# Splitting a load into 11 and 5 rows and holding back the first store in a rotary-embedding kernel on one core

## The chip, the cores and the metric

The kernel runs on one core of one Trainium2 chip. The metric is the device time of one execution in microseconds (us). Three runs of the kernel before gave 161.13, 161.54 and 161.68 us, with a median of 161.54 us.

## What is computed

The input `x` has the shape batch 16, sequence 512, heads 16, dim 64 in fp32. Of every head's 64 values, the first 32 are rotated by position-dependent factors and the last 32 are passed through. In the first 32, the quarters of 16 are the pair:

```python
x1, x2 = x[..., :32], x[..., 32:]
first  = x1[..., :16] * cos[..., :16] - x1[..., 16:] * sin[..., :16]
second = x1[..., :16] * sin[..., :16] + x1[..., 16:] * cos[..., :16]
out = concatenate([first, second, x2], axis=-1)
```

`cos` and `sin` are tables of 512 x 32, of which the first 16 columns are used. So 33.6 MB are read and 33.6 MB are written, and the arithmetic is four products, one difference and one sum for each rotated pair.

## The kernel before, in words

The 16 x 512 positions are cut into T = 4 tiles. Each tile holds 128 partitions x K = 16 positions, called rows here, of 16 heads x 64 values; a row of one partition is 4 KB, a tile is 8.4 MB. The buffer `ring` has room for NS = 3 tiles in SBUF, so tile 3 takes the place of tile 0 and can be loaded only when tile 0 has been stored. A tile is loaded into the buffer, its first half of every head is rotated in place, and the whole tile is stored, passed-through values included.

All loads and the stores of tiles 0, 1 and 3 are issued by SP (SyncE), in the order of the program: `load` (line 55) and `store` (line 58). The store of tile 2 is issued by POOL (GpSimd), which has a queue of its own. An issuing engine stops at an instruction that has to wait, and what stands behind it in the program waits too. On SP the order is: load 0, load 1, rows 8-16 of tile 2, store 0, rows 0-8 of tile 2, load 3, store 1, store 3.

The factors are loaded by two small transfers (lines 63 and 64), spread over partitions and repeated by VectorE (lines 73 to 86), until 21 us. From then on VectorE rotates. `rotate(t, lo, hi)` works on rows lo to hi of tile t, with four instructions: a multiplication by the sines into `b_t` in PSUM (line 96), a multiplication by the cosines in place (line 97), a subtraction for the first quarter (line 98) and an addition for the second (line 101). `b_t` has one buffer of KC = 8 rows, so no call takes more than 8 rows.

The order of the calls is written out by hand. Tiles 0, 1 and 3 are rotated in two calls of 8 rows. Tile 2 is rotated in rows 8-16, then 0-5 (KM = 5), then 5-8. Store 1 has an added dependency: it is held back until the addition of `rotate(2, 0, KM)`, called `near`, has ended, although tile 1 itself is ready earlier.

Of the kernel before, what the change touches and what calls it, by code (L numbers as in the profile page):

```python
# [1 line left out]

# [4 lines left out]


@with_exitstack
def kernel(  # L10
    ctx: ExitStack,
    tc: tile.TileContext,
    x: bass.AP,
    cos: bass.AP,
    sin: bass.AP,
    out: bass.AP,
):
    nc = tc.nc
    fp32 = mybir.dt.float32
    P = 128  # L20
    B, S, H, D = x.shape
    Q = D // 4
    HF = D // 2

    K = 16
    T = B * S // (P * K)
    PB = S // K
    REP = P // PB  # L30
    R = H * D
    NS = 3
    KC = K // 2
    KM = 5

    xf = x.rearrange("b s h d -> (b s h d)").rearrange("(t p f) -> t p f", t=T, p=P)
    of = out.rearrange("b s h d -> (b s h d)").rearrange("(t p f) -> t p f", t=T, p=P)
    cosf = cos.rearrange("(p k) j -> p (k j)", k=K)
    sinf = sin.rearrange("(p k) j -> p (k j)", k=K)

    const_pool = ctx.enter_context(tc.tile_pool(name="const", bufs=1))
    b_pool = ctx.enter_context(tc.tile_pool(name="bp", bufs=1, space=bass.MemoryType.PSUM))


    ring = const_pool.tile([P, NS, K, H, D], fp32)
    stage = const_pool.tile([P, 2, K, HF], fp32)
    spun = const_pool.tile([P, 2 * K, Q], fp32)
    packed = const_pool.tile([PB, 2 * K, Q], fp32)
    table = const_pool.tile([P, 2, K, 2, Q], fp32)

    def rows(t, lo, hi):
        return ring[:, t % NS, lo:hi].rearrange("p k h d -> p (k h d)")

    def load(t, lo=0, hi=K):
        return nc.sync.dma_start(out=rows(t, lo, hi), in_=xf[t, :, lo * R : hi * R])

    def store(t, lo=0, hi=K, queue=nc.sync):
        return queue.dma_start(out=of[t, :, lo * R : hi * R], in_=rows(t, lo, hi))  # L58


    nc.vector.memset(stage[:, :, :, 0:Q], 0.0)  # L61
    spread = stage.rearrange("(j b) t k i -> j b t (k i)", b=REP)
    nc.gpsimd.dma_start(out=spread[:, 0, 0], in_=cosf)  # L63
    nc.gpsimd.dma_start(out=spread[:, 0, 1], in_=sinf)  # L64
    load(0)
    load(1)
    load(2, KC, K)

    PQ = PB // REP
    nc.vector.stream_shuffle(  # L73
        out=spun[:],
        in_=stage.rearrange("p t k j -> p (t k) j")[:, :, 0:Q],
        mask=[j % PQ * REP for j in range(PB)],
    )
    for q in reversed(range(REP)):
        n = PQ * (q + 1)
        nc.vector.tensor_copy(out=packed[0:n], in_=spun[q * PB : q * PB + n])  # L80

    for r in range(REP):
        nc.vector.tensor_copy(  # L83
            out=table[r * PB : (r + 1) * PB].rearrange("p t k c j -> p (t k) c j"),
            in_=packed.unsqueeze(2).to_broadcast((PB, 2 * K, 2, Q)),
        )
    C = table[:, 0].rearrange("p k c j -> p k (c j)")
    Sn = table[:, 1].rearrange("p k c j -> p k (c j)")

    def rotate(t, lo, hi):  # L90
        x1 = ring[:, t % NS, lo:hi, :, 0:HF]
        c = C[:, lo:hi].unsqueeze(2).to_broadcast((P, hi - lo, H, HF))
        s = Sn[:, lo:hi].unsqueeze(2).to_broadcast((P, hi - lo, H, HF))
        b_full = b_pool.tile([P, KC, H, HF], fp32, name="b_t")
        b_t = b_full[:, 0 : hi - lo]
        nc.vector.tensor_mul(out=b_t, in0=x1, in1=s)  # L96
        nc.vector.tensor_mul(out=x1, in0=x1, in1=c)  # L97
        nc.vector.tensor_sub(  # L98
            out=x1[:, :, :, 0:Q], in0=x1[:, :, :, 0:Q], in1=b_t[:, :, :, Q:HF]
        )  # L100
        return nc.vector.tensor_add(  # L101
            out=x1[:, :, :, Q:HF], in0=x1[:, :, :, Q:HF], in1=b_t[:, :, :, 0:Q]
        )

    rotate(0, 0, KC)
    rotate(0, KC, K)
    store(0)
    load(2, 0, KC)
    load(3)
    rotate(1, 0, KC)  # L110
    rotate(1, KC, K)
    behind_loads = store(1)
    rotate(2, KC, K)
    near = rotate(2, 0, KM)
    rotate(2, KM, KC)
    store(2, queue=nc.gpsimd)

    tc.add_manual_dep(
        behind_loads.ins,
        near.ins.name,  # L120
        mybir.DependencyInfo(mybir.DependencyClass.Sync, mybir.DependencyReason.DATA),
        reason="the store follows the loads at the DMA engines",
    )
    rotate(3, 0, KC)
    rotate(3, KC, K)
    store(3)


# [1 line left out]
_INS = ['x', 'cos', 'sin']  # L130
_OUTS = [((16, 512, 16, 64), 'float32')]


# [23 lines left out]
```

## Time and profile before

| | |
|---|---|
| median of three runs | 161.54 us (161.13 to 161.68) |
| span of the profiled execution, first to last instruction | 159.5 us |
| median of the runs less that span | 2.04 us |
| VectorE busy | 112.9 us |
| POOL busy | 1.9 us |
| bytes moved | 67.24 MB, 422 GB/s over the span |
| store 0 issued | 49.92 us |
| store 1 issued | 98.90 us |
| store 2 issued (POOL) | 104.62 us |
| store 3 issued | 131.24 us |

The times in the lower half count from the first instruction of the profiled execution. The span is what the profiler saw between the first and the last instruction; the time of a run holds some more around it. In the profile DVE is VectorE and SPq is SP's instruction stream with its DMA issues; q1 is the queue that SP's transfers take and q0 that of POOL's. A DMA issue in a timeline is short: it hands the transfer over, and the transfer itself is seen in the DMA views and in the records of single packets.

### The profile page before, as it was taken

The page shows a single profiled execution, that of the slowest core. Times are in us where ns is not written, and L with a number is a line of the kernel's source. Part 1 is how long each engine was busy: PE and PEld are TensorE (multiplying, and loading weights), DVE is VectorE, ACT ScalarE, POOL GpSimd, SP SyncE. Part 2 cuts the span into 40 slices and gives each one's busy share as a digit, 9 for nine tenths or more (in the row PEclk, how much of TensorE's full clock was granted, in tenths as well). Part 3 has the DMA queues.
Part 4 walks back from the last instruction along what each step waited for, and adds up shares of the span by engine and source line. Part 5 has one row for each costly group of instructions (what it writes and reads, how often), then busy time and mean ns, then how long its engine had stood idle before and what let it go on. Part 6 is the DMA issues. An engine that isn't in the chain of part 4 may idle for free.

```text
span 159.5 us, 115 instructions
## 1 busy us (share of the span) xinstructions
DVE 112.9 (71%) x47; POOL 1.9 (1%) x7
## 2 busy tenths in 40 slices
DVE  1000959999999999999999999999999990000000
POOL 3000000000000000000000000010000000000000
DMA  7969979799699699699996996996996997999966
GB/s 263 542 263 542 444 345 526 345 444 526 271 493 551 279 510 526 263 394 411 510 526 263 526 526 263 526 526 263 526 526 263 526 460 329 526 394 394 526 263 263
DMA packets 1360, 67.24 MB, mean 422 GB/s; under 512 B 176, under 2 KB 176, under 8 KB 208
## 3 DMA queue, kind: packets, MB, share of 16 engines
q1 hardware_dynamic: 1152, 58.72, 85.7%
q0 software_dynamic: 208, 8.52, 12.4%
HBM read 33.69 MB, written 33.55 MB: 422 GB/s over the span
## 4 chain that ended last, share of the span: by engine, by line
DVE 61%; DMA 14%; issue 5%; DVEq 1%
DVE b_t L96 22%; DVE ring L97 22%; DMA ring<-in_x_dram 14%; DVE ring L101 10%; DVE ring L98 7%; DVEq L152 1%; DVEq L96 0%
## 5 line engine op out<-in xcount | busy, mean ns | idle before, releaser
L96 DVE TENSOR_TENSOR b_t<-ring,table 128x4096 f32<-128x4096 f32 (+2 forms) x9 | 35.6, 3959 | 2.1 <-DMA ring<-in_x_dram 1.8
L97 DVE TENSOR_TENSOR ring<-ring,table 128x4096 f32<-128x4096 f32 (+2 forms) x9 | 35.5, 3950 | 0.3
L98 DVE TENSOR_TENSOR ring<-ring,b_t 128x2048 f32<-128x2048 f32 (+2 forms) x9 | 18.4, 2049 | 0.3
L101 DVE TENSOR_TENSOR ring<-ring,b_t 128x2048 f32<-128x2048 f32 (+2 forms) x9 | 18.4, 2043 | 0.0
L73 DVE LOAD_MASK_SELECT spun<-stage x1 | 0.0, 14 | 14.4 <-DMA stage<-in_sin_dram 14.4
L83 DVE COPY table<-packed 32x1024 f32<-32x1024 f32 x4 | 2.7, 684 | 0.1
L58 POOL DMA_DIRECT2D out_dram<-ring x1 | 0.6, 562 | 101.7 <-DVE ring L101 101.7
L80 DVE COPY packed<-spun 32x512 f32<-32x512 f32 (+3 forms) x4 | 1.7, 416 | 0.1
L61 DVE MEMSET stage<- 128x512 f32 x1 | 0.5, 485 | 0.9 <-PEq L141 0.9
L73 DVE STREAM_SHUFFLE spun<-stage 128x512 f32<-128x512 f32 x1 | 0.7, 721 | 0.0
L63 POOL DMA_DIRECT2D stage<-in_cos_dram x1 | 0.6, 644 | 1.3 <-DVE stage L61 1.3
L64 POOL DMA_DIRECT2D stage<-in_sin_dram x1 | 0.5, 535 | 0.0
L141 POOL MEMSET const-bfloat16-1.0<- 128x1 bf16 x1 | 0.1, 102 | 0.0
L141 POOL MEMSET const-float32-0.0<- 128x1 f32 x1 | 0.1, 99 | 0.2 <-issue 0.2
L141 POOL MEMSET const-float32-1.0<- 128x1 f32 x1 | 0.1, 99 | 0.0
L141 POOL MEMSET const-uint8-127<- 128x1 uint8 x1 | 0.1, 99 | 0.0
## 6 DMA issues: line engine op xcount, KB each, us to landing
ring<-in_x_dram SPq DMA_DIRECT2D x2, 4096.0 KB, 40.7
stage<-in_cos_dram POOLq DMA_DIRECT2D x1, 64.0 KB, 9.0
stage<-in_sin_dram POOLq DMA_DIRECT2D x1, 64.0 KB, 13.3
ring<-in_x_dram SPq DMA_DIRECT2D x3, 29.0
out_dram<-ring SPq DMA_DIRECT2D x3, 27.4
out_dram<-ring POOLq DMA_DIRECT2D x1, 39.5
```

The costliest lines, as they stand in the source:

```text
L58: return queue.dma_start(out=of[t, :, lo * R : hi * R], in_=rows(t, lo, hi))
L61: nc.vector.memset(stage[:, :, :, 0:Q], 0.0)
L63: nc.gpsimd.dma_start(out=spread[:, 0, 0], in_=cosf)
L64: nc.gpsimd.dma_start(out=spread[:, 0, 1], in_=sinf)
L73: nc.vector.stream_shuffle(out=spun[:], in_=stage.rearrange("p t k j -> p (t k) j")[:, :, 0:Q], mask=[j % PQ * REP for j in range(PB)],)
L80: nc.vector.tensor_copy(out=packed[0:n], in_=spun[q * PB : q * PB + n])
L83: nc.vector.tensor_copy(out=table[r * PB : (r + 1) * PB].rearrange("p t k c j -> p (t k) c j"), in_=packed.unsqueeze(2).to_broadcast((PB, ...
L96: nc.vector.tensor_mul(out=b_t, in0=x1, in1=s)
L97: nc.vector.tensor_mul(out=x1, in0=x1, in1=c)
L98: nc.vector.tensor_sub(out=x1[:, :, :, 0:Q], in0=x1[:, :, :, 0:Q], in1=b_t[:, :, :, Q:HF])
L101: return nc.vector.tensor_add(out=x1[:, :, :, Q:HF], in0=x1[:, :, :, Q:HF], in1=b_t[:, :, :, 0:Q])
L152: with _tile.TileContext(nc) as tc:
```

## The change

Tile 2 is loaded as rows 5-16 (11 rows) ahead of store 0 and rows 0-5 (5 rows) behind it, instead of 8 and 8 rows. Tile 1 is rotated in calls of 7, 5 and 4 rows instead of 8 and 8. Store 0 gets an added dependency: it is held back until the first multiplication of tile 1 (line 96, over 7 rows) has ended. Tile 2 is rotated in rows 8-16, 3-8, 0-3 instead of 8-16, 0-5, 5-8; store 1 is held back, as before, until the addition of the second of these calls, which has 5 rows in both kernels. `rotate` now returns its first and its last instruction.

```diff
-    KM = 5
+    KA = 5
...
-    load(2, KC, K)
+    load(2, KA, K)
...
-        nc.vector.tensor_mul(out=b_t, in0=x1, in1=s)
+        first = nc.vector.tensor_mul(out=b_t, in0=x1, in1=s)
...
-        return nc.vector.tensor_add(
+        last = nc.vector.tensor_add(
             out=x1[:, :, :, Q:HF], in0=x1[:, :, :, Q:HF], in1=b_t[:, :, :, 0:Q]
         )
+        return first, last
...
-    store(0)
-    load(2, 0, KC)
+    first_store = store(0)
+    load(2, 0, KA)
     load(3)
-    rotate(1, 0, KC)
-    rotate(1, KC, K)
-    behind_loads = store(1)
-    rotate(2, KC, K)
-    near = rotate(2, 0, KM)
-    rotate(2, KM, KC)
+    begun, _ = rotate(1, 0, 7)
+    rotate(1, 7, 12)
+    rotate(1, 12, 16)
+    second_store = store(1)
+    rotate(2, 8, 16)
+    _, near = rotate(2, 3, 8)
+    rotate(2, 0, 3)
     store(2, queue=nc.gpsimd)
...
-    tc.add_manual_dep(
-        behind_loads.ins,
-        near.ins.name,
-        mybir.DependencyInfo(mybir.DependencyClass.Sync, mybir.DependencyReason.DATA),
-        reason="the store follows the loads at the DMA engines",
-    )
+    for behind, point in ((first_store, begun), (second_store, near)):
+        tc.add_manual_dep(
+            behind.ins,
+            point.ins.name,
+            mybir.DependencyInfo(mybir.DependencyClass.Sync, mybir.DependencyReason.DATA),
+            reason="the store follows the loads at the DMA engines",
+        )
```

## The prediction

> **What bounds the kernel now.** I read the page first, then the stretches, then the order of time around the waits that the change touches.
>
> The page's head, engine part and DMA queues:
>
> ```profile
> span 159.5 us, 115 instructions
> ...
> DVE 112.9 (71%) x47; POOL 1.9 (1%) x7
> ...
> DMA packets 1360, 67.24 MB, mean 422 GB/s; under 512 B 176, under 2 KB 176, under 8 KB 208
> ...
> q1 hardware_dynamic: 1152, 58.72, 85.7%
> q0 software_dynamic: 208, 8.52, 12.4%
> ```
>
> VectorE (DVE) is busy for 71% of the span, the two DMA queues for 85.7 + 12.4 = 98.1%. The kernel moves 67.24 MB and has hardly a moment in which the 16 DMA engines rest. The chain of waits gives VectorE 61%, but it stops at 131 us, where the last store is issued, and does not see that this store then stands behind other transfers. The view of stretches (columns: stretch, its us, VectorE busy, POOL busy, clock, DMA share, GB/s) shows the same:
>
> ```profile
> 4.00:50.00 46.00, 31.89 (x19) 0.00 (x0) 1.00 0.99 427
> ...
> 72.00:99.80 27.80, 27.52 (x12) 0.00 (x0) 1.00 1.00 434
> 99.80:158.20 58.40, 31.14 (x12) 0.56 (x1) 1.00 1.00 431
> ```
>
> The reader is to see a DMA share of 1.00 up to 158.2 us. So a step can cost time only where it lets the DMA engines run empty, and can gain time only where they do. A packet of 64 KB takes 2.418 us in the trace's packet records, 16 engines make 434 GB/s, and one row of a tile (128 x 4 KB = 0.524 MB) is 1.209 us of DMA. By those records the order on SP's queue is: tiles 0, 1 and half of 2 until 51.6; store 0 until 71.3; the other half of tile 2; tile 3 until 100.26; store 1, with store 2 (POOL's queue) beside it from 109.6; store 3 until 158.2.
>
> The place that matters is where store 1 takes over from the load of tile 3. The timeline (start, us, engine, line, operation):
>
> ```profile
> 90.26 2.83 DVE L96 TENSOR_TENSOR b_t<-ring,table 128x2560 f32<-128x2560 f32 x1
> 93.13 2.82 DVE L97 TENSOR_TENSOR ring<-ring,table 128x2560 f32<-128x2560 f32 x1
> 95.99 1.49 DVE L98 TENSOR_TENSOR ring<-ring,b_t 128x1280 f32<-128x1280 f32 x1
> 97.39 1.48 DVE L101 TENSOR_TENSOR ring<-ring,b_t 128x1280 f32<-128x1280 f32 x1
> 98.90 0.34 SPq L58 DMA_DIRECT2D out_dram<-ring  x1
> 98.91 1.77 DVE L96 TENSOR_TENSOR b_t<-ring,table 128x1536 f32<-128x1536 f32 x1
> ```
>
> The awaited addition ends at 97.39 + 1.48 = 98.87, SP issues store 1 at 98.90. The DMA view of 99 to 101 us in 40 slices of 0.05 us (a packet's bytes are counted where it starts) shows when the 16 engines pass from load to store:
>
> ```profile
> GB/s 0 0 0 0 0 0 0 0 0 0 0 0 0 0 0 0 0 1311 1311 6554 2622 2622 0 1311 3932 1311 0 0 0 0 0 0 0 0 0 0 0 0 0 0
> ```
>
> The first 17 slices are empty, since every engine is inside its last load packet; store 1's packets start from 99.88 to 100.26. In the records the first engine ends its load at 99.86 and takes a store packet at 99.88, 0.98 us after the issue. The only issue into empty queues, load 0, gives nearly the same: issued at 0.74, first packet at 1.75, 1.01 us. So the time from issue to first packet is about 0.98 us, and store 1 arrives just as the engines come free: **its margin is about zero.**
>
> **The change part by part.**
>
> *Tile 1 in 7, 5 and 4 rows instead of 8 and 8.* Four VectorE instructions more. From starts in the timeline, a chunk of 8 rows takes 49.93 - 36.48 = 13.45 us, of 5 rows 98.91 - 90.26 = 8.65, of 3 rows 104.36 - 98.91 = 5.45. That is a line: 0.65 us a chunk and 1.60 us a row. So 7, 5, 4 rows take 11.85 + 8.65 + 7.05 = 27.55 us against 26.90: **+0.65 us.** All that VectorE does later is 0.65 us later, as it waits for no DMA after 23.03 us. The awaited addition in tile 2 is the same instruction at the same place (rows 8-16, then 3-8), so store 1 is issued at 98.90 + 0.65 = 99.55 and its first packet can start at 99.55 + 0.98 = 100.53, where the engines are free from 99.86. From there to the end lie stores 1, 2, 3, 48 rows x 1.209 = 58.0 us of DMA (99.88 to 158.2 now): whatever delays the first packet moves the end. +0.65 on the path.
>
> *Store 2 and store 3 are issued 0.65 later too* (105.27 and 131.9). Both are covered: store 1 fills the engines when store 2 is issued (its first packet waits until 109.6 now); when store 3 is issued, store 2 still has 12 us to go, and store 3's first packet starts only at 136.18. Cost 0. Without store 2 as cover each would cost 0.65.
>
> *The load of tile 2 as 11 and 5 rows.* Bytes are the same, so the loads of tile 3 end where they did. The trace has no packet of 44 or 20 KB. The 32 KB packet takes 1.213 us and the 64 KB one 2.418, so the fixed part is 0.008 us a packet, and the number of packets stays at 8 an engine. Bounds from -0.01 to +0.01 us: 0. Both parts land in time: 11 rows 3 x 1.209 = 3.63 us later than 51.6 and needed near 77.5; rows 0-5 at 81.4 as now and needed at about 90.9.
>
> *The wait of store 0.* It is put behind the first multiplication over 7 rows. From the rows 4433, 2833 and 1767 ns for 4096, 2560 and 1536 elements (1.042 ns an element), 3584 elements take 3.90 us: end at 53.83, issue at 53.86 instead of 49.92, first packet possible at 54.84. The 11 rows keep the engines busy until 50.97 + 3.63 = 54.60 on the first and 51.59 + 3.63 = 55.22 on the last. So there are 0 to 0.24 us of rest on single engines, 0.05 on the mean. It does not add up with the 0.65: it shifts the loads, and store 1 is held by VectorE until 100.53 anyway. Behind store 0 on SP are the 5 rows (issued near 54.3, their turn near 74.8) and tile 3, which waits for store 0's landing as before; it would be issued near 75.7 with the 5 rows' 6.05 us still in the queue. Cost 0 unless over 0.65.
>
> *The restart of an engine that has rested* is the unknown. Bounds: store packets that follow loads without a rest (51.0 us) take 2.418 to 2.427, no excess; load packets into cold engines (1.75 us) take 2.98 to 3.39, up to 0.97 excess. I take 0, since the rest is short and the packet is a store, and keep +0.97 for the range.
>
> Against the 0.98 us speaks the Trainium skill, "DMA: Bandwidth & Descriptors", Latency and other measured facts: a queue of this kind delivers its first byte some 0.6 us after the issue. Counted from the issue at 0.74, the trace shows 1.01 instead; by the page's figure, an estimate, store 1 would have had 0.38 us of margin and the change would cost 0.27 us.
>
> Sum: span 159.5 + 0.65 = 160.15. The median of the runs, 161.54, lies 2.04 us above the profiled span; with the same surroundings 162.19.
>
> **The rivals.**
>
> **A (forecast, 0.58): store 1 comes 0.65 us late and the whole tail moves.** 162.2 us, +0.4%.
>
> **B (0.20): the margin is larger than I read it.** 0.98 us is an upper bound where the engines were busy, and the 1.01 us of the first load may hold a cold start. For it: no engine rests between load and store now. Against it: the first two store packets at 99.88 and 99.93 are longer than the rest (2.460 and 2.434 against 2.418 us), as if just in time. The time from issue to packet lies between the 0.34 us that SP spends on the issue itself and 0.98, so the margin lies between 0.64 and 0 and the cost between 0.01 and 0.65; from the middle, 0.33: 161.9 us.
>
> **C (0.15), not slower: the switch from store 0 to the load of tile 2.** In the records the last packets of store 0 (67.9 to 71.25 us) take up to 3.33 us and the first load packets up to 1.40 instead of 1.21, together 0.43 us an engine on the mean and up to 0.9 on one. If the later store 0 or the shorter first load piece takes that away, tile 3 is in 0.43 to 0.9 us earlier. It decides only if the time from issue to packet is under 0.3 us, since store 1 is issued at 99.55 and has to be there before 99.86; both rows, 0.98 and 1.01, speak against that. Then 160.6 to 161.1 us; I take 161.0.
>
> **D (0.07): the restart costs its cold price** at store 1, up to 0.97 us: 162.7 to 163.2, I take 163.0.
>
> That the change does not do what it says is possible for store 0 alone: if the 11 rows end before it arrives, it follows with a gap; of no weight for the end, as above.
>
> **How the numbers follow.** The time is A's, 162.2. The range 161.1 to 162.9 takes in A and B and the edges of C and D; about 0.15 is left out. A measurement of this kernel can tell about 0.3%, 0.48 us, from no change, so slower begins at 162.02 and faster ends at 161.06. Slower: 0.53 of A, 0.03 of B, 0.07 of D = 0.63. Same: 0.05 of A, 0.17 of B, 0.05 of C = 0.27. Faster: 0.10 of C.
>
> **What would show it.** In the timeline after, store 0 issued near 53.9, store 1 near 99.55 and store 3 near 131.9; in the DMA view of 99 to 101 us a hole of about 0.65 us before store 1's packets, which start near 100.5; a span near 160.15. B would show packets near 100.2. C would show last packets of store 0 at 2.42 us and the load of tile 3 in before 99.6. The forecast is wrong if the tail from store 1's first packet is not 58.3 us, or if VectorE's tile 1 is not 27.55 us.

## The result and the profile after

The changed kernel takes 163.49 us (four runs, 163.21 to 163.89) against 161.51 us (four runs, 161.13 to 161.68): 1.0122 times as long, 95% interval 1.0104 to 1.0139. It is 1.98 us slower, where the prediction had +0.65 and at most +1.4 in its range. The profiled execution has a span of 161.3 us against 159.5.

VectorE did what was forecast, to 0.02 us. The timeline of the changed kernel (start, us, engine, line, operation), first VectorE at the start of tile 1, at the start of tile 2 and at the awaited addition, then SP (a line with x2 takes two issues together, and its time runs from the first to the end of the second):

```profile
49.95 3.90 DVE L96 TENSOR_TENSOR b_t<-ring,table 128x3584 f32<-128x3584 f32 x1
...
77.49 4.43 DVE L96 TENSOR_TENSOR b_t<-ring,table 128x4096 f32<-128x4096 f32 x1
...
98.06 1.48 DVE L101 TENSOR_TENSOR ring<-ring,b_t 128x1280 f32<-128x1280 f32 x1
```

```profile
53.87 0.35 SPq L58 DMA_DIRECT2D out_dram<-ring  x1
54.26 22.23 SPq L55 DMA_DIRECT2D ring<-in_x_dram  x2
99.57 32.68 SPq L58 DMA_DIRECT2D out_dram<-ring  x2
```

Tile 1 takes 77.49 - 49.95 = 27.54 us (27.55 forecast), store 0 is issued at 53.87 (53.86), store 1 at 99.57 (99.55). But the hole ahead of store 1 is not there. The DMA view of 101 to 103 us in slices of 0.05 us:

```profile
GB/s 1311 6554 0 2622 0 1311 1311 0 0 0 1311 0 1311 0 0 0 2622 0 0 0 0 0 2622 0 0 0 0 0 0 0 0 0 0 0 0 0 0 0 0 0
```

Store 1's packets start from 101.04 to 102.14, not at 100.53, and they start the moment each engine ends its last load packet. Store 1 had been issued 1.47 us before the first of them. The loads came late, and they came spread over 1.1 us where it was 0.4 before. So the time was lost earlier, and VectorE's 0.65 us lie hidden under it.

The page's queue lines and the stretches of the changed kernel, which answer to those shown of before:

```profile
DMA packets 1360, 67.24 MB, mean 417 GB/s; under 512 B 176, under 2 KB 176, under 8 KB 208
...
q1 hardware_dynamic: 1152, 58.72, 85.3%
q0 software_dynamic: 208, 8.52, 12.2%
```

```profile
4.00:50.00 46.00, 31.87 (x19) 0.00 (x0) 1.00 0.98 423
72.00:99.80 27.80, 27.49 (x13) 0.00 (x0) 1.00 1.04 434
99.80:158.20 58.40, 31.80 (x12) 0.56 (x1) 1.00 0.99 431
```

The queues' share of the span went from 98.1 to 97.5%: 0.6% of 161.3 us, about 1 us, are rests and the time in which engines that have ended wait for the slowest. The other microsecond hides in engines that count as busy. Each transfer ends on each engine with a 4-byte write, and the packet records hold all of these. Their means over the 16 engines cut the time into transfers (us; the ideal is rows x 1.209):

| stage | before | after | ideal in after | lost more in after |
|---|---|---|---|---|
| 8 or 11 rows of tile 2 | 9.68 | 13.63 | 13.30 | 0.32 |
| store 0 | 19.67 | 20.21 | 19.34 | 0.54 |
| 8 or 5 rows of tile 2 | 9.76 | 6.66 | 6.05 | 0.53 |
| load of tile 3 | 19.31 | 19.32 | 19.34 | 0 |
| stores 1, 2, 3 | 58.02 | 57.98 | 58.03 | 0 |

The last column compares what each load cost beyond its rows in the two kernels. The three losses are 1.39 us; tile 1 ended 0.05 earlier, so the mean engine ends its loads 1.35 us later. The slowest ends them 1.88 us later (102.14 against 100.26) and the last store as well (160.09 against 158.21): the spread between engines makes up the other half microsecond.

Within these stages the packet records of the changed kernel show, as means over 16 engines: 0.19 us of rest ahead of store 0 (its first packet came 1.36 us after the issue; the records do not name the engine, so a single engine's rest is only known to lie between 0 and 0.63 us), 0.63 us in store 0's last packets (before: 0.35), 0.18 us of rest behind them (0.01), and 0.45 us in the 5-row load (0.10). The place where the engines pass from store 0 to the load behind it is called the turn from here on. Its DMA view, 9 us in slices of 0.225 us, first before (67 to 76 us), then after (71 to 80 us):

```profile
GB/s 0 0 0 291 874 2330 1165 0 0 0 0 0 0 0 0 0 583 874 874 0 0 0 1019 728 583 0 0 146 1456 728 0 0 0 1165 1019 146 0 0 291 1311
DMA packets 107, 3.51 MB, mean 390 GB/s; under 512 B 16, under 2 KB 16, under 8 KB 16
```

```profile
GB/s 0 0 0 0 0 2621 1748 291 0 0 0 0 0 0 0 0 0 0 182 273 637 91 273 273 728 182 364 637 364 182 637 455 91 182 819 364 182 728 364 273
DMA packets 123, 2.91 MB, mean 324 GB/s; under 512 B 16, under 2 KB 16, under 8 KB 16
```

The reader is to see the gap between the starts of store 0's last packets and those of the first load packets: 9 empty slices before, 10 after. A packet of 64 KB that takes its usual 2.42 us fills 10.7 slices from start to start, and these last packets start over only three or four slices, so without a loss some 7 slices would be empty. The records give these packets up to 3.33 us before and 3.51 after. After the gap the load comes in thin, uneven slices. The rates over the same length tell it in one number: 390 and 324 GB/s. A packet counts whole where it starts, so a turn without loss does not reach 434 over so short a stretch: the cheap turn with the wait after 4 rows, shown below, has 401.

### The profile page after: what moved, and what is told of

Same layout as the page of the kernel before. It is cut to its first block, busy times and chain, and to the rows that moved or that the text cites. A ratio compares the mean times of both kernels' runs of the same rounds, so it can differ in the third digit from the quotient of the medians.

```text
span 161.3 us, 119 instructions
## 1 busy us (share of the span) xinstructions
DVE 113.4 (70%) x51; POOL 1.9 (1%) x7
## 4 chain that ended last, share of the span: by engine, by line
DVE 62%; DMA 14%; issue 4%; DVEq 1%
DVE b_t L96 22%; DVE ring L97 22%; DMA ring<-in_x_dram 14%; DVE ring L101 10%; DVE ring L98 7%; DVEq L155 1%; DVEq L96 0%
## 5 line engine op out<-in xcount | busy, mean ns | idle before, releaser
L96 DVE TENSOR_TENSOR b_t<-ring,table 128x4096 f32<-128x4096 f32 (+4 forms) x10 | 35.8, 3580 | 2.2 <-DMA ring<-in_x_dram 1.9
L97 DVE TENSOR_TENSOR ring<-ring,table 128x4096 f32<-128x4096 f32 (+4 forms) x10 | 35.7, 3571 | 0.3
L98 DVE TENSOR_TENSOR ring<-ring,b_t 128x2048 f32<-128x2048 f32 (+4 forms) x10 | 18.6, 1860 | 0.3
L101 DVE TENSOR_TENSOR ring<-ring,b_t 128x2048 f32<-128x2048 f32 (+4 forms) x10 | 18.5, 1854 | 0.0
```

What stands on the lines that cost most here:

```text
L96: first = nc.vector.tensor_mul(out=b_t, in0=x1, in1=s)
L98: nc.vector.tensor_sub(out=x1[:, :, :, 0:Q], in0=x1[:, :, :, 0:Q], in1=b_t[:, :, :, Q:HF])
L101: last = nc.vector.tensor_add(out=x1[:, :, :, Q:HF], in0=x1[:, :, :, Q:HF], in1=b_t[:, :, :, 0:Q])
```

## The experiments

All times are medians of the timed runs, each compared with runs of the kernel before on the same chip (161.48 to 161.59 us in the four sets).

The first four take the change apart. Two theories were on record: H, that the wait of store 0 makes the turn dear, and S, that loads in packets of these sizes are slow by themselves.

**Without the wait of store 0**

```diff
-    for behind, point in ((first_store, begun), (second_store, near)):
+    for behind, point in ((second_store, near),):
```

> The changed kernel without the added wait of store 0; the 11 and 5 rows and the calls of 7, 5, 4 rows stay. In the changed kernel the packet records show, as means over 16 engines, 0.32 us more in the 11-row load, 0.19 us of rest ahead of store 0, 0.28 us more in store 0's last packets, 0.18 us of rest and 0.35 us more in the 5-row load. Theory H (the hold: store 0 reaches engines that have run empty, all start it together and so all turn from store to load together, which makes the turn dear): the rest ahead of store 0 and the dear turn go, loads end 0.3 us later than before, store 1 is then held by VectorE at 99.55 us: about 162.0 to 162.2 us. Theory S (the sizes: loads in 44 KB and 20 KB packets are slow by themselves): only the rest of 0.19 us goes; about 163.2 us.

Measured: 162.38 us (162.09 to 162.61), 1.0053 (1.0040 to 1.0066). Store 0 is issued as early as in the kernel before:

```profile
49.93 0.35 SPq L58 DMA_DIRECT2D out_dram<-ring  x1
```

The wait is worth 1.1 us, more than theory S allows and less than H. The rest ahead of store 0 is gone and the turn behind it too: its last packets lose 0 and the 5-row load 0.11 us. But something new appeared: the last packets of the 11-row load, just ahead of store 0, lose 0.38 us.

**Only tile 1 in three calls**, in the kernel before:

```diff
-    rotate(1, 0, KC)
-    rotate(1, KC, K)
+    rotate(1, 0, 7)
+    rotate(1, 7, 12)
+    rotate(1, 12, 16)
```

> The kernel before with tile 1 rotated in calls of 7, 5, 4 rows and nothing else changed. Both theories leave this term as the prediction had it: VectorE 0.65 us later, store 1 issued at 99.55 us, a rest of 0.65 us ahead of its first packet near 100.53 us, 162.2 us. If an issue into empty queues takes longer than 0.98 us (store 0 in the changed kernel took 1.36 us), the first packet comes near 100.9 us and the time is near 162.6 us. If store 1 had margin, 161.9 us or less.

Measured: 162.00 us (161.86 to 162.14), 1.0032 (1.0020 to 1.0043). This is the prediction's main term by itself, +0.52 instead of +0.65 us. The DMA view of 99 to 101 us of this kernel shows the hole:

```profile
GB/s 0 0 0 0 0 0 0 0 0 0 0 0 0 0 0 0 0 0 0 0 0 0 0 0 0 0 9175 5243 5243 1311 0 0 0 0 0 0 0 0 0 0
```

All 16 engines start store 1 between 100.31 and 100.46, together, where they had ended the load between 99.88 and 100.21. Store 1 was issued at 99.47, so the first packet comes 0.84 us after the issue where the engines have come to rest by then. By this figure the kernel before had 0.14 us of margin, not zero.

**Only the load split**, in the kernel before:

```diff
-    load(2, KC, K)
+    load(2, 5, K)
...
-    load(2, 0, KC)
+    load(2, 0, 5)
```

> The kernel before with tile 2 loaded as 11 and 5 rows and nothing else changed: no wait for store 0, tile 1 in two calls of 8 rows. Theory S: the 11-row load loses 0.32 us, the turn from store 0 to the 5-row load and that load lose 0.8 us more than before on the mean, and the slowest engine some 0.5 us more: about 163.0 us. Theory H: only the 11-row load's 0.32 us, 161.8 us.

Measured: 162.19 us (162.04 to 162.48), 1.0042 (1.0030 to 1.0054), between the two theories. As without the wait, the turn behind store 0 is cheap (0), and the last packets of the 11-row load lose 0.48 us; its other packets lose 0.30.

**The wait put behind 4 instead of 7 rows**

```diff
-    begun, _ = rotate(1, 0, 7)
-    rotate(1, 7, 12)
-    rotate(1, 12, 16)
+    begun, _ = rotate(1, 0, 4)
+    rotate(1, 4, 11)
+    rotate(1, 11, 16)
```

> The changed kernel with tile 1 in calls of 4, 7, 5 rows, so that the point that store 0 waits for comes after 4 rows: the multiplication takes 2.30 us, store 0 is issued near 52.3 us, 2.7 us ahead of the first engine's end of the 11-row load. All of VectorE's later times stay. Theory H: no rest ahead of store 0 and a turn as cheap as before, 162.0 to 162.2 us. Theory S: about 163.2 us, as without the wait.

Measured: 161.97 us (161.92 to 162.08), 1.0026 (1.0015 to 1.0038). The same loads, calls of the same three sizes in another order, a wait of the same kind that ends 1.6 us earlier: 1.5 us less. Store 0 was issued at 52.25, 2.65 us ahead of the first engine's end of the load:

```profile
52.25 0.35 SPq L58 DMA_DIRECT2D out_dram<-ring  x1
```

The DMA view of 71 to 80 us of this kernel, to be held against the one of the changed kernel above:

```profile
GB/s 0 0 0 1165 2330 1165 0 0 0 0 0 0 0 0 273 819 364 273 546 364 273 455 637 364 273 819 182 182 546 637 182 364 819 273 273 637 455 91 546 728
DMA packets 157, 3.61 MB, mean 401 GB/s; under 512 B 16, under 2 KB 16, under 8 KB 16
```

8 empty slices instead of 10, and 401 GB/s instead of 324 over the same stretch with the same 5-row packets. Both turns together lose 0.07 us on the engine's mean. What is left of the time over the kernel before is VectorE's: the engines rest 0.50 us ahead of store 1. Theory H gave the right time, but its reason (all engines turn together) did not explain the slow load packets of the two runs with store 0 issued early. Theory L took its place: that the lead of store 0 decides, the time from its issue to the end of the first engine's load in front of it.

**9 and 7 rows in the kernel before, with a lead of 2.2 us and no wait; and the same with store 1 issued 1.5 us earlier**

```diff
-    load(2, KC, K)
+    load(2, 7, K)
...
-    load(2, 0, KC)
+    load(2, 0, 7)
```

> The kernel before with tile 2 loaded as 9 and 7 rows and nothing else changed. Theory L (lead): what decides is how long ahead of the end of the loads in front of it store 0 is issued. With 1.1 us of lead (kernel before, changed kernel) the last packets of store 0 are slow (0.35 and 0.63 us an engine), with 5 us (split only, no wait) the last load packets ahead of it (0.38 and 0.48), with 2.7 us (the hold after 4 rows) neither (0.07 together). Here the lead is 2.3 us without any hold: both turns cheap, loads end some 0.3 us earlier; store 1, issued at 98.90 and at the engines 0.84 to 0.98 us later, takes up nearly all of it: 161.3 to 161.5 us. Theory C (chance, or the sizes of the packets): a turn of some 0.4 us stays, 161.5 to 161.9 us.

> The same 9 and 7 rows, and the point that store 1 waits for comes after 4 instead of 5 rows of tile 2 (KM = 4), so that store 1 is issued at 97.3 us. Theory L: the 0.3 us of the turn reach the end, 161.1 to 161.2 us. Theory C: 161.5 to 161.8 us.

(the second with `KM = 4`). Measured: 161.73 us, 1.0005 (0.9996 to 1.0014), and 161.83 us, 1.0011 (1.0001 to 1.0022). Both miss the 161.1 to 161.5 us of theory L. The turns are cheap as it said, 0.16 and 0.08 us for both sides together, but the packets of the 9-row load lose 0.14 and 0.33 us well before the turn. That is the 11-row loss again, for a load of another odd number of rows.

**12 and 4 rows in the changed kernel**

```diff
-    KA = 5
+    KA = 4
```

> The changed kernel with tile 2 loaded as 12 and 4 instead of 11 and 5 rows; the hold after 7 rows and the calls of 7, 5, 4 rows stay. The loads ahead of store 0 end 1.21 us later, so that store 0, issued at 53.87 us as in the changed kernel, has a lead of 2.3 us instead of 1.1. Theory L: no rest ahead of store 0, cheap turns, store 1 held by VectorE at 99.57 us: 162.0 us. If the hold itself, the calls of 7, 5, 4 or small packets behind store 0 were the cause, 163.5 us or more.

Measured: 161.97 us (161.82 to 162.21), 1.0021 (1.0012 to 1.0030), as theory L said. The wait is the one of the changed kernel, issued at 53.92; one row more ahead of it takes the 1.5 us away. The 48-KB packets lose 0.02 us.

**The wait put behind 6 rows**

```diff
-    begun, _ = rotate(1, 0, 7)
-    rotate(1, 7, 12)
-    rotate(1, 12, 16)
+    begun, _ = rotate(1, 0, 6)
+    rotate(1, 6, 11)
+    rotate(1, 11, 16)
```

> The changed kernel with tile 1 in calls of 6, 5, 5 rows, so that store 0 is issued near 53.34 us, 0.53 us earlier: a lead of 1.65 us instead of 1.12. Store 0's first packet came 1.36 us after the issue in the changed kernel, so there is no rest ahead of store 0. Theory L: a turn behind store 0 between those of leads 1.1 and 2.7 us, 0.1 to 0.4 us; store 1 held by VectorE: 162.0 to 162.3 us. If the rest ahead of store 0 has nothing to do with the dear turn: 163.2 us.

Measured: 161.97 us, and 1.0046 (1.0024 to 1.0068) over all runs. Twelve runs of one kernel fall into two groups: eight lie from 161.86 to 162.03, four from 162.65 to 163.63. The one profiled, of the first group, shows a lead of 1.80 us and a turn of 0.05 us. No trace of the four longer ones was kept, so that they are executions with a dear turn is likely and not shown.

**10 and 6 rows in the changed kernel**, so that store 0 comes when the loads are over:

```diff
-    KA = 5
+    KA = 6
```

> The changed kernel with tile 2 loaded as 10 and 6 rows: the loads ahead of store 0 end 1.21 us earlier, near 53.8 us, when store 0 is issued (53.87 us): lead about zero, and a rest of 0.9 to 1.4 us ahead of store 0 on every engine instead of 0 to 0.6. Theory F (a store 0 that reaches empty engines brings the dear turn to the load behind it, whatever the rest): the turn of the changed kernel stays and the longer rest is added, 164.3 to 164.8 us. Theory G (the dear turn comes only from arriving while some engines have ended and others have not, which spreads them): the rest alone, loads end near 101.3 us, 162.5 to 163.0 us.

Measured: 162.99 us (162.85 to 163.11), 1.0086 (1.0073 to 1.0099). The DMA view of 54 to 56 us (slices of 0.05 us), of this kernel and then of the changed one:

```profile
GB/s 0 0 0 0 0 0 0 0 0 0 0 0 0 0 0 0 5243 6554 6554 2621 0 0 0 0 0 0 0 0 0 0 0 0 0 0 0 0 0 0 0 0
```

```profile
GB/s 0 0 0 0 0 0 0 0 0 0 0 0 0 0 0 0 0 0 0 0 0 0 0 0 1311 5243 3932 1311 2622 1311 2621 1311 1311 0 0 0 0 0 0 0
```

With a mean rest of 1.16 us, and at least 0.7 on every engine, the store starts on all of them within 0.14 us, 0.85 us after its issue; in the changed kernel it starts over 0.4 us, 1.36 to 1.75 us after its issue, with a mean rest of 0.19 us. Theory F is right on the trace: store 0's last packets lose 0.76 us. Theory G is right on the time: it is 0.5 us *less* than the changed kernel's although the rest is a microsecond longer, since the 10-row load loses nothing where the 11-row load lost 0.33, the load behind store 0 loses 0.13 instead of 0.45 us, nothing rests behind the store, and the engines end the loads within 0.4 us of each other instead of 1.1. Neither theory covers both.

**13 and 3 rows, tile 1 in two calls of 8, with and without the wait** (the kernel without it also leaves `(first_store, begun)` out)

```diff
-    KA = 5
+    KA = 3
...
-    begun, _ = rotate(1, 0, 7)
-    rotate(1, 7, 12)
-    rotate(1, 12, 16)
+    begun, _ = rotate(1, 0, 8)
+    rotate(1, 8, 16)
```

> Tile 2 loaded as 13 and 3 rows, tile 1 in two calls of 8 rows as in the kernel before (no 0.65 us of VectorE), store 0 held until the first multiplication over 8 rows: issued near 54.4 us, lead 2.8 us. Theory L (lead): cheap turns on both sides, no rest ahead of store 0, loads end at or a little ahead of the kernel before; store 1 issued at 98.9 us: 161.2 to 161.6 us. If a hold costs by itself, or 3 rows behind store 0 are too few: 162 us or more.

> The same 13 and 3 rows without the hold of store 0: issued at 49.92 us, lead 7.2 us. Theory L: the last load packets ahead of store 0 are slow, as with leads of 5 us (0.38 and 0.48 us an engine): 161.8 to 162.2 us. If a long lead costs nothing: the same time as with the hold.

Measured: 162.66 us (162.01 to 163.73) and 163.12 us (162.85 to 164.61). Both are above what was expected. The medians differ by about half a microsecond in the direction of theory L, but the runs overlap, so that the wait helps here is not clear of noise. The traces show the sides that theory L names: 0.23 us in the last load packets ahead of store 0 with a lead of 3.3 us, 0.65 with 8.0. But the 52-KB packets lose 0.36 and 0.22 us as other odd row counts do, and single engines lose up to 1.06 us at the start of tile 3, so that the loads end spread over 2.4 us with the wait (its profiled run is its slowest, 163.73 us) and over 1.5 us without. Why they do with 3 rows and not with 4 stays open.

**Which of the two issues makes the turn dear.** Store 0 and the load behind it are always issued 0.39 us apart, so an early or late store is also an early or late load. Holding that load separately, until the addition of tile 1's first call, parts them:

```diff
-    load(2, 0, KA)
+    second_load = load(2, 0, KA)
...
-    begun, _ = rotate(1, 0, 7)
+    begun, seven = rotate(1, 0, 7)
...
+    for behind, point in ((first_store, begun), (second_load, seven), (second_store, near)):
```

> The changed kernel with the load of the last 5 rows of tile 2 held as well, until the addition of tile 1's first call has ended: issued near 61.8 us, 13 us ahead of its turn, instead of 0.39 us behind store 0. Theory L1 (store 0's own lateness brings the dear turn): the last packets of store 0 and the 5-row load stay slow, 163.2 to 163.9 us. Theory L2 (the load that is put into the queues while they are nearly empty does): the turn is cheap, only the rest ahead of store 0 stays, store 1 held by VectorE, 162.0 to 162.3 us.

> The changed kernel with store 0 not held (issued at 49.93 us, lead 5 us) and the 5-row load held as in the run before this one (61.8 us). Without the second hold the last packets of the 11-row load lost 0.38 us and the time was 162.38 us. Theory L1 (store 0's own early issue makes the last load packets ahead of it slow): 162.3 to 162.5 us again. Theory L2 (the load queued behind it does): store 1 held by VectorE, 162.0 us.

(the second leaves `(first_store, begun)` out). Measured: 163.55 us (163.44 to 163.75) and 162.32 us (162.13 to 162.71). Neither moves from the 163.49 and 162.38 us without the second hold. The load's issue does not matter; the store's own does, as theory L1 had it.

**12 and 4 rows, tile 1 in two calls of 8, with and without the wait**, the cleanest pair: the same bytes, the same VectorE work as the kernel before, the wait alone differs (the second leaves `(first_store, begun)` out).

```diff
-    KA = 5
+    KA = 4
...
-    begun, _ = rotate(1, 0, 7)
-    rotate(1, 7, 12)
-    rotate(1, 12, 16)
+    begun, _ = rotate(1, 0, 8)
+    rotate(1, 8, 16)
```

> Tile 2 loaded as 12 and 4 rows, tile 1 in two calls of 8 rows (no 0.65 us of VectorE), store 0 held until the first multiplication over 8 rows: issued near 54.4 us, lead 1.8 us. The 48 KB packets of the 12 rows lost only 0.02 us. Lead theory: 0.05 to 0.2 us of turn, loads end near 99.6 to 100.1 us, store 1 issued at 98.9 us: 161.2 to 161.6 us, the kernel before or a little less. If a hold of store 0 costs by itself: above 162 us.

> The same 12 and 4 rows and calls of 8 rows without the hold of store 0: issued at 49.92 us, lead 6.2 us. Lead theory: the last load packets ahead of store 0 lose 0.4 to 0.65 us, 161.8 to 162.2 us. If the length of a lead above 2 us does not matter and the 13-row kernels lost by their packets alone: the same as with the hold.

Measured: 161.55 us (161.07 to 161.86), 0.9994 (0.9980 to 1.0007), and 162.57 us (162.32 to 162.62), 1.0055 (1.0038 to 1.0072). SP's timeline of the first and of the second:

```profile
54.47 0.35 SPq L58 DMA_DIRECT2D out_dram<-ring  x1
54.86 22.05 SPq L55 DMA_DIRECT2D ring<-in_x_dram  x2
98.99 32.68 SPq L58 DMA_DIRECT2D out_dram<-ring  x2
```

```profile
49.90 0.35 SPq L58 DMA_DIRECT2D out_dram<-ring  x1
50.29 27.58 SPq L55 DMA_DIRECT2D ring<-in_x_dram  x2
98.88 32.68 SPq L58 DMA_DIRECT2D out_dram<-ring  x2
```

Issuing the store 4.6 us *later* saves 1.0 us. Unheld, the last load packets ahead of it lose 1.03 us an engine. The held version is the best of those with a wait, and equals the kernel before; no version tried beats it.

All leads side by side (us from store 0's issue to the first engine's end of the load ahead of it; losses in ns, means over 16 engines; "behind" is store 0's last packets and the rest after them):

| lead | kernel | ahead of store 0 | behind it | rest before store 0 |
|---|---|---|---|---|
| -0.50 | 10 and 6 rows | 3 | 768 | 1162 |
| 1.05 | before | 4 | 360 | 2 |
| 1.12 | changed | 4 | 807 | 185 |
| 1.26 | changed, load held too | 3 | 718 | 134 |
| 1.45 | 12 and 4, wait after 8 | 8 | 196 | 3 |
| 1.54 | tile 1 in three calls | 22 | 113 | 2 |
| 1.80 | wait after 6 rows | 16 | 46 | 2 |
| 1.87 | 12 and 4 in the changed | 12 | 141 | 2 |
| 2.24 | 9 and 7 | 20 | 139 | 3 |
| 2.55 | 9 and 7, store 1 early | 10 | 72 | 2 |
| 2.65 | wait after 4 rows | 44 | 27 | 2 |
| 3.29 | 13 and 3, wait | 232 | 3 | 2 |
| 5.47 | no wait | 376 | 2 | 2 |
| 5.52 | no wait, load held | 220 | 3 | 2 |
| 5.55 | split only | 477 | 2 | 2 |
| 7.03 | 12 and 4, no wait | 1029 | 0 | 2 |
| 7.97 | 13 and 3, no wait | 649 | 8 | 2 |

Too short a lead is paid behind the store, too long a lead ahead of it. Between 1.54 and 2.65 us both sides together cost 0.06 to 0.16 us in these traces. Each row is one profiled execution, and a lead is no guarantee: of the twelve runs with the row of 1.80, four were long, while all twelve with the row of 1.45 were not.

That the lead is a cause is shown by pairs that leave the rest of the kernel alone: the changed kernel with and without the wait (1.12 and 5.47 us), 12 and 4 rows with and without it (1.45 and 7.03). VectorE does the same in both kernels of each pair. The wait after 4 rows against 7 also changes the order of the calls, and 11 against 12 rows, under an unmoved issue, also the size of the packets.

The lead is not the whole cause. The kernel before and the changed kernel have nearly the same one, 1.05 and 1.12 us: the wait moved store 0's issue by 3.95 us, and the three rows more, with what they lost, moved the first engine's end of the load by 4.02. Yet they lose 0.36 and 0.81 us behind the store. What differs between them is the rest ahead of store 0: 2 and 185 ns. The three kernels with such a rest are the three that lose most behind the store, 0.72 to 0.81 us, and a rest six times as long (10 and 6 rows) did not cost more there. No run changes this rest alone, so that it makes the turn dear is not shown. Why store 0 took 1.36 us to reach the engines, which made the rest, and what happens inside an engine is not shown either.

## Why the prediction was wrong

*What bounds the kernel* was half right. DMA sets the time, and losses ahead of store 1 move the whole tail one to one: stores 1, 2, 3 took 57.98 us on the mean engine, 58.0 by the rows. But the sentence "a step can cost time only where it lets the DMA engines run empty" was false. Of the 1.39 us that the mean engine lost, 0.35 were rest (0.18 ahead of store 0 and 0.17 behind it, both less what they were before); the rest was packets that took longer, and an engine in a long packet counts as busy. The stretch from 72 to 99.8 us does not show the loss in its share (1.04) or in its rate, 434 GB/s as before; the durations of packets and the times from one transfer's end to the next do.

*Tile 1 in three calls*: VectorE's 0.65 us was exact, its price alone 0.52 us since the margin was 0.14 instead of zero (0.84 us from issue to packet instead of 0.98). In the changed kernel it cost nothing, because the loads came later still.

*11 and 5 rows* were costed at 0 from the durations of 32- and 64-KB packets. The 44-KB packets lost 0.32 us more than the 32-KB ones. The row counts show a pattern, whose cause is open: the first load of tile 2 lost 0.14 to 0.46 us away from the turn in the eleven traces with 9, 11 or 13 rows, and 0.01 to 0.15 us in the six with 8, 10 or 12. The duration of a packet of another size was interpolated where nothing had measured it.

*The wait of store 0* is **the step that failed**: "Cost 0 unless over 0.65". It allowed for the rest before store 0, put at 0.05 us on the mean and measured at 0.19, and for nothing behind it. The first packet was forecast for 54.84 and came at 55.23. The store's own last packets, 20 us later, the rest behind them and the 5-row load then lost another 0.8 us over the kernel before. With the wait taken out, the time fell by 1.1 us. Rival C had named exactly this place, with 0.43 us already lost there before, but only asked whether that loss could vanish. It grew, and its growth was larger than every term of the sum. Rival D's mechanism, a dear first packet after a rest, did not occur: the first packets of store 0 took 2.43 to 2.47 us, 0.04 over the usual.

*The spread of the engines* was missing from the sum. It worked on the first and the mean engine, while the slowest ends the kernel: 0.53 of the 1.88 us. One of the prediction's own signs of being wrong shows it: from store 1's first packet to the end it took 59.05 us (101.04 to 160.09) instead of 58.3, although the mean engine took no longer.

*The covers* for stores 2 and 3 held; POOL issued store 2 at 105.29 (105.27 forecast), with no rest behind it. The 0.65 us on these two cost nothing.

## What to carry to other kernels

When a queue passes from loads to a store, the store's place in time matters although the queue runs in order. Here, with 11 rows ahead of the store, the kernels took 163.49 us with a lead of 1.12 us, 161.97 with 2.65 and 162.38 with 5.47; with 12 rows, 161.55 with 1.45 and 162.57 with 7.03. A place in the profile where time is already lost, such as the 0.43 us behind store 0, is to be costed as something that can grow, not only go. And where a busy share is full, look at the durations of single packets and at the times between the ends of transfers before calling a step free.

## What the runs showed of the hardware

Counted from the start of SP's issue, which itself takes 0.34 to 0.35 us, the first packet came after 0.84 to 0.86 us in nine kernels in which the engines had come to rest by then: store 0 with 10 and 6 rows, and store 1 in eight others, among them tile 1 in three calls, the wait after 4 rows and no wait. In all of them the first engine ended its load at most 0.74 us after the issue. With 1.10 to 1.26 us it took longer although engines rested: store 0 took 1.36 us in the changed kernel and in the one with the second load held, store 1 took 1.19 us with 13 and 3 rows and the wait. The kernel before, with 1.05 us, shows at most 1.06 us for store 0 and no rest. Why these differ is open. The Trainium skill ("DMA: Bandwidth & Descriptors", Latency and other measured facts) has about 0.6 us to the first byte for such a queue; no issue here came under 0.84.

The same section gives 0.2 us on average and 2 us at high load for an access to HBM. Whether such accesses have a part in the packets that lengthen at the turns, no run here shows.

The first load of tile 2 lost more with odd numbers of 4-KB rows (packets of 36, 44 and 52 KB: 0.14 to 0.46 us in a load) than with even ones (32, 40 and 48 KB: at most 0.15 us). The seven traces with the same 11 rows alone range from 0.14 to 0.46.
